# Score products over 128 rows, and pairs of 64-row products issued side by side, in a two-block transformer kernel

## The chip, the core and the metric

The kernel runs on one core of one Trainium2 chip. The metric is device time in microseconds (us) for one execution. A core has a matrix engine (TensorE, in the profile PE, its weight loads PEld), a vector engine (DVE), a scalar engine (ACT), a general engine (POOL), and a queue that issues most transfers (SP). Each engine takes its instructions in the order in which the program has them.

A matrix product reads a stationary operand ("weights", loaded first) and a moving operand. Both lie on up to 128 partitions ("rows"), over which the product sums; the moving operand streams its columns. In the profile `64*128 64x512` is a product over 64 rows with 128 weight columns and 512 moving columns.

## The reference, cut to what matters

Two layers of a first block and one layer of a second, on 512 tokens of width 1024, in float32. Each layer is FFN, mixer, FFN. The mixer of the first block has four groups of four heads of width 64; these three have products over 64 rows:

```
nsa:    s = (q @ k.T) + bias, causal; softmax; o = p @ v        (two branches, and a small compressed one)
gdn:    per chunk of 128 tokens:  K = k @ k.T ,  Q = q @ k.T ,  masked and scaled
mlstm:  S = q @ k.T ;  w = exp(-(M - a)) ;  o = (S * w) @ v ,  causal blocks of 128 tokens
```

The mixer of the second block has 16 heads: 8 "dilated" heads with scores of 128 x 512 per block of 128 queries, and 8 "neighbourhood" heads with scores of 128 x 256.

## The kernel before

Matrix products in float32 run in two ways. Most split each operand into a high part and a rest (`hi`, `lo`, type float32r) and multiply hi*hi, lo*hi and hi*lo, one pass each (`mm3`, lines 308, 311 and 312). Some stay plain float32; the chip runs each of those as two passes, so the profile shows two matrix instructions for one of the program.

**Scores of nsa (lines 1532 and 1533) and of the second block (lines 1708 and 1709).** One head has 64 rows. The first product of a score uses all 128: the query tile holds the high part of a head in one half of its rows and the rest in the other, and the key tile holds the key's high part twice, so one product gives hi*hi + lo*hi. The second product adds q-hi * k-lo and reads only the 64 rows that hold the query's high part. In the second block `parts` (lines 1608 to 1626) makes these tiles: `split` writes `hl`, and four transfers on SP's queue (line 1625) copy halves of it into `two`. The second product reads `hl` itself.

**mlstm (line 1337).** For each head, and each of four key blocks j, one plain float32 product over 64 rows with 512, 384, 256 or 128 columns. Heads 0 and 2 lie on rows 0 to 63, heads 1 and 3 on rows 64 to 127. Heads follow each other.

**gdn (lines 1149 to 1158).** For each chunk and each half u of the rows, four plain float32 products of 64 rows by 128 columns; half 1 comes after half 0.

These parts are Python generators that `par` steps in turn, together with projections that are independent of them. The generators' order gives priorities, and a scheduler fixes each engine's order from priorities, dependences and free buffers. PSUM has two banks for tag `mm` and six for tag `a`, which holds every other product's result.

Of the kernel before, what the change touches and what calls it, by code (L numbers as in the profile page):

```python
# [225 lines left out]
def _body(tc, nc, ctx, I, out):  # L226
# [10 lines left out]
    def nm(s):  # L237
        cnt[0] += 1
        return f"{s}{cnt[0]}"
# [850 lines left out]
    def gdn(blkr, l, MX, m_, n_, q_, s_, c_, t_, out_split, pr, cv, ga, beta, lvl):  # L1090
# [44 lines left out]
        def chunk(c):  # L1135
# [10 lines left out]
            QK[c], BT[c] = m_("qk"), m_("bt")  # L1146
            bs = BT[c]
            g = (V if c < 2 else G).tensor_tensor(q4(bs), q4(seg), b_last(su(beta[:, c]), 128), op=ALU.mult)
            for u in range(2):
                pk = psa()  # L1150
                r = slice(64 * u, 64 * u + 64)
                for b in range(2):
                    PE.matmul(pk[:, b * 128:b * 128 + 128], kT[b][r, ts], kT[b][r, ts], start=True, stop=True)
                    PE.matmul(pk[:, 256 + b * 128:256 + b * 128 + 128], kT[b][r, ts], qT[b][r, ts], start=True,
                              stop=True)
                us = slice(256 * u, 256 * u + 256)
                V.tensor_tensor(bs[:, us], pk[:, 0:256], bs[:, us], op=ALU.mult)
                V.tensor_tensor(QK[c][:, us], pk[:, 256:512], seg[:, us], op=ALU.mult)
                yield
# [127 lines left out]
    def mlstm(sel2, l, MX, m_, n_, q_, s_, c_, t_, out_split, pr, vd, gt, lf):  # L1287

        pi, pf = psa(), psa()
        for i in range(4):  # L1290
            PE.transpose(pi[0:4, i * 128:i * 128 + 128], gt[:, i, 20:24], ident)
            PE.transpose(pf[0:4, i * 128:i * 128 + 128], lf[:, i], ident)
        rw, rM, nF = n_("rw")[0:36], n_("rM")[0:4], n_("nF")[0:4]
        V.memset(rw, 0.0)
        V.tensor_tensor_scan(nF, ones[0:4, 0:1].to_broadcast([4, 512]), pf[0:4, :], 0.0, op0=ALU.mult, op1=ALU.add)
        a = rw[0:4, :]
        V.tensor_tensor(a, pi[0:4, :], nF, op=ALU.add)
        V.tensor_tensor_scan(rM, a, a, 0.0, op0=ALU.max, op1=ALU.max)
        V.tensor_tensor(rw[32:36, :], nF, rM, op=ALU.subtract)
        rr = n_("rr", F32R)[0:36]  # L1300
        S.activation(rr, ones[0:36, 0:1].to_broadcast([36, 512]), AF.Copy, scale=0.0)
        split(rr[0:4], rr[32:36], rM)
        yield
        pc = psa()
        for i in range(4):
            PE.transpose(pc[:, i * 36:i * 36 + 36], rw[:, i * 128:i * 128 + 128], ident[0:36, 0:36])
        ac = t_([128, 4, 36], "ac")
        V.tensor_copy(ac.rearrange("p i r -> p (i r)"), pc[:, 0:144])
        em = t_([128, 4, 4], "em")
        act(em, ac[:, :, 32:36], AF.Exp)  # L1310
        while "d_q1" not in pr:
            yield
        dk, dq = ([pr[f"d_{c}{b}"] for b in range(2)] for c in "kq")
        hn = [n_("hn"), n_("hn")]
        hv = [h_.rearrange("p (i e) -> p i e", i=2) for h_ in hn]
        for h in range(4):
            r, b = slice(64 * (h % 2), 64 * (h % 2) + 64), h // 2
            sel = MX.tile([36, 128], F32R, tag="s", bufs=4, name=nm("sel"))
            V.tensor_copy(sel, b_last(sel2[:, h], 128))
            ps = psa("pM")  # L1320
            PE.matmul(ps, sel, rr, start=True, stop=True)
            pM = n_("pM")
            S.copy(pM, ps)
            yield
            dA, dB, dC = n_("d"), n_("d"), q_("d")
            wt = [dA, dB[:, 0:384], dC, dB[:, 384:512]]
            for j in range(4):
                n = 512 - 128 * j
                aj = ac[:, j, h:h + 1]
                d = wt[j]  # L1330
                V.scalar_tensor_tensor(d[:, 0:128], pM[:, j * 128:j * 128 + 128], aj, mmask, op0=ALU.subtract,
                                       op1=ALU.max)
                act(d[:, 0:128], d[:, 0:128], AF.Exp, scale=-1.0)
                if n > 128:
                    act(d[:, 128:n], pM[:, (j + 1) * 128:512], AF.Exp, scale=-1.0, bias=aj)
                ps = psa("S")
                PE.matmul(ps[:, 0:n], dk[b][r, j * 128:j * 128 + 128], dq[b][r, j * 128:512], start=True, stop=True)  # L1337
                V.scalar_tensor_tensor(d[:, 0:n], ps[:, 0:n], 0.125, d[:, 0:n], op0=ALU.mult, op1=ALU.mult)
                yield
            pn = psa("num")  # L1340
            for i in range(4):
                for j in range(i + 1):
                    PE.matmul(pn[:, i * 65:i * 65 + 65], wt[j][:, (i - j) * 128:(i - j) * 128 + 128], vd[:, j, h],  # L1343
                              start=j == 0, stop=j == i)
            yield
            pv = pn[:, 0:260].rearrange("p (i e) -> p i e", e=65)
            de = c_([128, 4, 2], "de")
            V.tensor_copy(de[:, :, 1], pv[:, :, 64])
            V.scalar_tensor_tensor(de[:, :, 0], de[:, :, 1], -1.0, de[:, :, 1], op0=ALU.mult, op1=ALU.max)
            V.tensor_tensor(de[:, :, 0], de[:, :, 0], em[:, :, h], op=ALU.max)  # L1350
            V.reciprocal(de[:, :, 0], de[:, :, 0])
            t = q_("hq").rearrange("p (i e) -> p i e", i=4)
            V.tensor_tensor(t, pv[:, :, 0:64], b_last(de[:, :, 0], 64), op=ALU.mult)
            q = q_("hq").rearrange("p (i e) -> p i e", i=4)
            S.activation(q, t, AF.Square)
            V.tensor_reduce(de[:, :, 0], q, axis=AX.X, op=ALU.add)
            rsq(de[:, :, 0], de[:, :, 0], 1.0 / 64)
            for g in range(2):
                V.tensor_tensor(hv[g][:, :, h * 64:h * 64 + 64], t[:, 2 * g:2 * g + 2],
                                b_last(de[:, 2 * g:2 * g + 2, 0], 64), op=ALU.mult)  # L1360
            yield
        for b in range(2):
            pt = psa()
            for i in range(4):
                PE.transpose(pt[:, i * 128:i * 128 + 128], hv[i // 2][:, i % 2, b * 128:b * 128 + 128], ident)
            S.activation(dq[b], pt, AF.Identity, scale=C(("mng", l)))
            yield
        while "gates" not in pr:
            yield
        for b in range(2):  # L1370
            out_split(6 + b, dq[b], pr[f"d_o{b}"])
# [48 lines left out]
    def nsa(blkr, l, MX, m_, n_, q_, s_, c_, t_, out_split, pr, hs, cw2, va, sg):  # L1420
# [70 lines left out]
        for h in range(4):  # L1491
# [34 lines left out]
            for br in range(2):  # L1526
                po = psa("o")
                for i in range(4):
                    n = 128 * (i + 1)
                    q = qa[b][:, h % 2, i * 128:i * 128 + 128]  # L1530
                    ps = psa("s")
                    PE.matmul(ps[:, 0:n], q, kk[br][0][:, 0:n], start=True, stop=False)
                    PE.matmul(ps[:, 0:n], q[r], kk[br][1][r, 0:n], start=False, stop=True)  # L1533
                    t = soft_e(n_, c_, ps, n, md[:, 512 - n:512])
                    late.add(unit_b(t, n, po, i, br))
                    if i == 3:
                        late.add(fin(po, h, br), True)
                    yield
# [40 lines left out]
    def _mix2(MX, q0, wf):  # L1579
# [33 lines left out]
        def parts(nat, key, q):  # L1613
            t = m_("qk")
            o, i, r = t, q, box["r"] if key else r8
            if nat and not key:
                o = t.rearrange("p (b r c) -> p r b c", b=4, r=8)
                i, r = (v.rearrange("p (r b c) -> p r b c", r=8, b=4) for v in (q, r))
            V.tensor_tensor(o, i, r, op=ALU.mult)
            hl_ = MX.tile([128, 2, 512], F32R, tag="hl", bufs=4, name=nm("hl"))  # L1620
            two = MX.tile([128, 2, 512], F32R, tag="two", bufs=4, name=nm("two"))
            split(hl_[:, 0], hl_[:, 1], t)
            for u in range(2):
                for v in range(2):
                    nc.sync.dma_start(two.bitcast(F32)[64 * v:64 * v + 64, u], hl_.bitcast(F32)[64 * u:64 * u + 64, 0 if key else u ^ v])
            return two, hl_

        def projv(half, v1, qs, ready=None):
            for c in range(4):
# [71 lines left out]
        late, nat = Late(3, 2), [0]  # L1701

        def scores(n, u, ts, keys, w, bias, nb=1):
            (qa, qh), (ka, kl) = pairs[n]
            r = slice(64 * u, 64 * u + 64)
            ps = psa("s")
            o = ps[:, 0:w] if nb == 1 else ps[:, 0:w].rearrange("p (a b) -> p a b", a=nb)
            PE.matmul(o, qa[:, u, ts], keys(ka[:, u]), start=True, stop=False)
            PE.matmul(o, qh[r, 0, ts], keys(kl[r, 1]), start=False, stop=True)  # L1709
            return soft_e(m_, s_, ps, w, bias)  # L1710

        def dilated():
# [180 lines left out]
```

## Time and profile before

| | us |
|---|---|
| median of 3 runs (lowest to highest) | 3311.61 (3310.05 to 3312.95) |
| the profiled execution: device time | 3313.13 |
| its span in the trace | 3311.4 |
| PE busy in the span | 3242.6 (98%) |
| DVE, ACT, POOL busy | 1723.8, 1212.6, 740.8 |

The granted clock is 0.991 of full speed over the span. A busy time counts overlapping instructions once. A matrix instruction's time contains its way through the array, during which the next one already starts; what it costs is therefore the step from its start to the start of the next, not its duration. The mixers of the first block fill about 508 to 715 us and 1617 to 1824 us of the span, the attention of the second block 2677 to 2880 us.

### The profile page before, as it was taken

How to read it: one execution, taken by the hardware profiler on the slowest of the kernel's cores; microseconds unless marked ns; L12 is line 12 of the kernel's file. 1: busy time of each engine (PE TensorE's matmuls, PEld its weight loads, DVE VectorE, ACT ScalarE, POOL GpSimd, SP SyncE). 2: the span in 40 equal slices, each digit the busy share in tenths (PEclk: the TensorE clock that was granted, in tenths of full speed). 3: DMA queues.
4: the chain of work that ended last, by engine and by line, in shares of the span. 5: the costliest groups of instructions: out<-in, count | busy, mean ns of one | idle time of the engine just before them, and what ended most of it. 6: DMA issues, size and time to landing. Idle time of an engine off the chain costs nothing.

```text
span 3311.4 us, 42958 instructions
## 1 busy us (share of the span) xinstructions
PE 3242.6 (98%) x16168; PEld 2690.1 (81%) x16168; DVE 1723.8 (52%) x2942; ACT 1212.6 (37%) x2287; POOL 740.8 (22%) x754
## 2 busy tenths in 40 slices
PE   7999999999999999999999999999999999999998
PEld 6888887778888888888877888888888877788887
DVE  6555576656555555536655633344543444564433
ACT  3222255453222232224444532233223444652232
POOL 3222222214222222213121322211211300131111
PEclk8999999999999999999999999999999999999999
DMA  6555542114555445534310334333323444342233
GB/s 235 183 167 173 175 143 72 33 45 139 167 168 165 154 143 176 164 117 132 111 34 30 109 100 134 120 118 105 128 97 98 135 148 118 99 139 97 96 94 104
DMA packets 133263, 410.77 MB, mean 124 GB/s; under 512 B 16264, under 2 KB 29708, under 8 KB 132784
## 3 DMA queue, kind: packets, MB, share of 16 engines
q1 hardware_dynamic: 126848, 387.07, 36.1%
q0 software_dynamic: 6064, 20.76, 2.0%
q8 instruction: 127, 2.08, 0.3%
q14 instruction: 80, 0.66, 0.1%
q10 hardware_dynamic: 144, 0.21, 0.0%
HBM read 379.58 MB, written 22.51 MB: 121 GB/s over the span
## 4 chain that ended last, share of the span: by engine, by line
PE 91%; DVE 5%; ACT 2%; issue 1%; POOL 1%; DMA 1%; SPq 0%; DVEq 0%; ACTq 0%; POOLq 0%
PE m L308 14%; PE m L311 14%; PE m L312 14%; PE a L308 11%; PE a L312 11%; PE a L311 11%; PE o L1397 2%; PE pt L1391 2%; DVE lo L297 1%; PE s L1709 1%; PE S L1337 1%; PE a L1191 1%; PE a L1175 1%; PE s L1533 1%; PE num L1343 1%
## 5 line engine op out<-in xcount | busy, mean ns | idle before, releaser
L297 DVE TENSOR_TENSOR lo<-raw,hi 128x512 fp32r<-128x512 f32 (+2 forms) x1056 | 804.9, 767 | 955.2 <-ACT hi L296 930.9
L296 ACT CAST hi<-raw 128x512 fp32r<-128x512 f32 (+2 forms) x1056 | 639.4, 611 | 1653.6 <-PE m L311 902.9
L308 PE MATMUL m<-hh,hi 128*128 128x512 f32 (+1 forms) x1728 | 668.7, 387 | 11.0 <-ACT hh L474 5.3
L311 PE MATMUL m<-hl,hi 128*128 128x512 f32 (+1 forms) x1728 | 661.8, 383 | 5.6 <-DVE hl L633 4.3
L312 PE MATMUL m<-hh,lo 128*128 128x512 f32 (+1 forms) x1728 | 659.8, 382 | 1.8 <-DVE lo L297 1.7
L311 PE MATMUL a<-hl,hi 128*128 128x512 f32 (+1 forms) x1264 | 476.5, 377 | 1.0 <-DVE hl L623 1.0
L308 PE MATMUL a<-hh,hi 128*128 128x512 f32 (+1 forms) x1264 | 476.6, 377 | 0.0
L312 PE MATMUL a<-hh,lo 128*128 128x512 f32 (+1 forms) x1264 | 475.2, 376 | 0.0
L308 PEld LDWEIGHTS m<-hh,hi 128*128 128x128 f32 x1728 | 327.5, 190 | 74.1 <-ACT hh L474 5.5
L311 PEld LDWEIGHTS m<-hl,hi 128*128 128x128 f32 x1728 | 327.4, 189 | 66.5 <-DVE hl L633 5.4
L312 PEld LDWEIGHTS m<-hh,lo 128*128 128x128 f32 x1728 | 327.3, 189 | 64.6 <-DVE lo L297 5.2
L717 POOL TENSOR_SCALAR uh<-u 128x512 fp32r<-128x512 f32 x132 | 112.6, 853 | 1099.9 <-DVE u L710 698.6
L311 PEld LDWEIGHTS a<-hl,hi 128*128 128x128 f32 x1264 | 240.1, 190 | 44.7 <-DVE hl L623 1.8
L312 PEld LDWEIGHTS a<-hh,lo 128*128 128x128 f32 x1264 | 239.9, 190 | 43.2 <-DVE lo L297 0.7
L308 PEld LDWEIGHTS a<-hh,hi 128*128 128x128 f32 x1264 | 240.1, 190 | 42.7 <-ACT hi L296 0.5
L308 PE MATMUL a<-uh,hi 128*128 128x512 f32 (+1 forms) x660 | 229.7, 348 | 0.6
L311 PE MATMUL a<-ul,hi 128*128 128x512 f32 (+1 forms) x660 | 229.5, 348 | 0.0
L312 PE MATMUL a<-uh,lo 128*128 128x512 f32 (+1 forms) x660 | 228.7, 347 | 0.0
L308 PE MATMUL m<-uh,hi 128*128 128x512 f32 x528 | 205.7, 390 | 0.0
L720 POOL TENSOR_TENSOR ul<-u,uh 128x512 fp32r<-128x512 f32 x132 | 203.1, 1538 | 10.8
L312 PE MATMUL m<-uh,lo 128*128 128x512 f32 x528 | 205.4, 389 | 0.0
L311 PE MATMUL m<-ul,hi 128*128 128x512 f32 x528 | 205.4, 389 | 0.0
(462 smaller groups left out, 4012.3 us busy)
## 6 DMA issues: line engine op xcount, KB each, us to landing
raw<-in_ada_dram SPq DMA_DIRECT2D x144, 512.0 KB, 4.3
raw<-in_f1a_dram SPq DMA_DIRECT2D x88, 512.0 KB, 4.2
raw<-in_f2a_dram SPq DMA_DIRECT2D x88, 512.0 KB, 3.7
raw<-in_win_dram SPq DMA_DIRECT2D x48, 512.0 KB, 3.3
raw<-in_g1a_dram SPq DMA_DIRECT2D x44, 512.0 KB, 3.7
raw<-in_g2a_dram SPq DMA_DIRECT2D x44, 512.0 KB, 3.6
raw<-in_f1b_dram SPq DMA_DIRECT2D x32, 512.0 KB, 3.6
raw<-in_f2b_dram SPq DMA_DIRECT2D x32, 512.0 KB, 3.5
```

The source lines that it names most:

```text
L296: order["hi"] = S.copy(h, raw[:, s])
L297: order["lo"] = V.tensor_tensor(l, raw[:, s], h.bitcast(F32), op=ALU.subtract)
L308: i = PE.matmul(o, wh, xh, start=start, stop=False)
L311: PE.matmul(o, wh, xl, start=False, stop=False)
L312: j = PE.matmul(o, wl, xh, start=False, stop=stop)
L717: G.tensor_scalar(uh[:, j], u, 1.0, 0.0, op0=ALU.mult, op1=ALU.add)
L720: order["ul"] = G.tensor_tensor(ul[:, j], u, uh[:, j].bitcast(F32), op=ALU.subtract)
L1175: PE.matmul(p[:, bs_], B[:, bs_], Z[:, bs_], start=True, stop=True)
L1191: PE.matmul(p[:, bs_], RT[:, bs_], w[:, bs_], start=True, stop=True)
L1337: PE.matmul(ps[:, 0:n], dk[b][r, j * 128:j * 128 + 128], dq[b][r, j * 128:512], start=True, stop=True)
L1391: PE.transpose(pt[:, j * 128:j * 128 + 128], t[:, j * 128:j * 128 + 128], ident)
L1397: PE.matmul(o, r[:, j * 128:j * 128 + 128], v, start=j == 0, stop=j == len(vs) - 1)
```

## The change

Second score products read all 128 rows: in nsa the key tile with the rest already held it in both halves; in the second block `parts` makes for each key one more tile, `low`, with four more transfers, and lays out every query as high part over rest. The added term lo*lo comes with it. Tiles `hl` have 2 buffers where they had 4, and `low` has 2. In gdn and mlstm, the products of two heads on the two halves of the rows are issued alternately, each half into a PSUM bank of its own; mlstm works on two heads at a time, with the exponentials of both in a step ahead of the two products, and on the weighted sums of one head after the other.

```diff
@@ gdn, chunk
+            pks = [psa(), psa()]
+            for b in range(2):
+                for o, x in ((0, kT), (256, qT)):
+                    for u in range(2):
+                        r = slice(64 * u, 64 * u + 64)
+                        PE.matmul(pks[u][:, o + b * 128:o + b * 128 + 128], kT[b][r, ts], x[b][r, ts], start=True, stop=True)
             for u in range(2):
-                pk = psa()
-                r = slice(64 * u, 64 * u + 64)
-                for b in range(2):
-                    PE.matmul(pk[:, b * 128:b * 128 + 128], kT[b][r, ts], kT[b][r, ts], start=True, stop=True)
-                    PE.matmul(pk[:, 256 + b * 128:256 + b * 128 + 128], kT[b][r, ts], qT[b][r, ts], start=True,
-                              stop=True)
+                pk = pks[u]
...
@@ mlstm (for each pair b of heads, for each j)
+                pss = [psa("S"), psa("S")]
+                for u in range(2):
+                    r = slice(64 * u, 64 * u + 64)
+                    PE.matmul(pss[u][:, 0:n], dk[b][r, j * 128:j * 128 + 128], dq[b][r, j * 128:512], start=True, stop=True)
+                for u in range(2):
+                    d = wts[u][j]
+                    V.scalar_tensor_tensor(d[:, 0:n], pss[u][:, 0:n], 0.125, d[:, 0:n], op0=ALU.mult, op1=ALU.mult)
+                yield
...
@@ nsa
-                    PE.matmul(ps[:, 0:n], q[r], kk[br][1][r, 0:n], start=False, stop=True)
+                    PE.matmul(ps[:, 0:n], q, kk[br][1][:, 0:n], start=False, stop=True)
...
@@ second block, parts
+            out_ = []
+            for g in range(2 if key else 1):
+                two = MX.tile([128, 2, 512], F32R, tag=("two", "low")[g], bufs=(4, 2)[g], name=nm("two"))
+                for u in range(2):
+                    for v in range(2):
+                        nc.sync.dma_start(two.bitcast(F32)[64 * v:64 * v + 64, u],
+                                          hl_.bitcast(F32)[64 * u:64 * u + 64, g if key else v])
+                out_.append(two)
...
@@ second block, scores
-            PE.matmul(o, qh[r, 0, ts], keys(kl[r, 1]), start=False, stop=True)
+            PE.matmul(o, qa[:, u, ts], keys(kl[:, u]), start=False, stop=True)
```

On PE, in the first mixer where mlstm's first products stand (`S`; `m` is a projection, `s` an nsa score), the program before has:

```order
L312 MATMUL m_5045<-hh,lo_5038 128x512
L1337 MATMUL S_5058<-d_q_4778,d_k_4456 128x512
L1532 MATMUL s_5061<-kk_4286,qa_4339 128x384
L1533 MATMUL s_5061<-kk_4287,qa_4339 128x384
L1397 MATMUL o_4783<-va_3728,pt_4952 128x65 x3
```

and the changed one, with line 1337 now 1344:

```order
L312 MATMUL m_5048<-hh,lo_5045 128x512
L1344 MATMUL S_5149<-d_q_4778,d_k_4456 128x512
L1344 MATMUL S_5150<-d_q_4778,d_k_4456 128x512
L1515 MATMUL a_5163<-kc_3970,a_q_4260 128x32 x4
L1201 MATMUL a_5174<-km,R_5020 128x128 x2
```

Two heads' products stand together. All 16 pairs of the two layers do; one instruction here is two passes on the chip.

On PE, in the second block at the first scores of the third pair of heads (`two_22859` and `two_22871` are the keys' high parts, `hl_22858` and `two_22876` their rests, `pt` are transposes, `o` weighted sums), the program before has:

```order
L1708 MATMUL s_22892<-two_22859,two_22814 128x512
L1709 MATMUL s_22892<-hl_22858,hl_22813 128x512
L1391 MATMUL pt_22899<-km,ts_22771 128x128 x4
L1397 MATMUL o_22731<-vdi_22009,pt_22791 128x65 x4
L1708 MATMUL s_22910<-two_22859,two_22814 128x512
L1709 MATMUL s_22910<-hl_22858,hl_22813 128x512
```

and the changed one:

```order
L1722 MATMUL s_22907<-two_22871,two_22826 128x512
L1402 MATMUL pt_22914<-km,ts_22781 128x128 x4
L1408 MATMUL o_22741<-vdi_22009,pt_22801 128x65 x4
L1722 MATMUL s_22925<-two_22871,two_22826 128x512
L1402 MATMUL pt_22932<-km,ts_22792 128x128 x4
L1408 MATMUL o_22741<-vdi_22009,pt_22812 128x65 x4
L1722 MATMUL s_22943<-two_22871,two_22826 128x512
L311 MATMUL m_23090<-hl,hi_23097 128x512
L312 MATMUL m_23090<-hh,lo_23098 128x512
L1723 MATMUL s_22907<-two_22876,two_22826 128x512
```

The second products of a pair's first scores have moved behind other work. It is so for six of the eight pairs; later scores of a pair have both products together.

On SP's queue, four more transfers stand after the four of each key's high parts, ahead of the next weights.

On PE, in gdn's chunks 0 and 1 (results: `a_4094` and `a_4104` are half 0 of chunk 0 and of chunk 1, `a_4117` and `a_4124` half 1), the program before has:

```order
L1154 MATMUL a_4094<-c_q_3474,c_k_3324 128x128
L1153 MATMUL a_4094<-c_k_3393 128x128
L1154 MATMUL a_4104<-c_q_3474,c_k_3324 128x128
L1154 MATMUL a_4094<-c_q_3576,c_k_3393 128x128
L1153 MATMUL a_4104<-c_k_3393 128x128
L1154 MATMUL a_4104<-c_q_3576,c_k_3393 128x128
L1154 MATMUL a_4117<-c_q_3474,c_k_3324 128x128
L1153 MATMUL a_4117<-c_k_3393 128x128
```

and the changed one (`a_4094` and `a_4095` are the halves of chunk 0, `a_4109` and `a_4110` those of chunk 1):

```order
L1154 MATMUL a_4094<-c_q_3474,c_k_3324 128x128
L1154 MATMUL a_4095<-c_q_3474,c_k_3324 128x128
L1154 MATMUL a_4094<-c_k_3393 128x128
L1154 MATMUL a_4095<-c_k_3393 128x128
L1154 MATMUL a_4094<-c_q_3576,c_k_3393 128x128
L1154 MATMUL a_4095<-c_q_3576,c_k_3393 128x128
L1154 MATMUL a_4109<-c_q_3474,c_k_3324 128x128
L1154 MATMUL a_4110<-c_q_3474,c_k_3324 128x128
```

The halves now alternate. Chunks 2 and 3, between which eleven rows of other work stood in the first layer, follow each other directly.

## Rows read from the trace of the kernel before

**Rows 1.** The page: busy time of each engine, and the chain that ended last

```profile
PE 3242.6 (98%) x16168; PEld 2690.1 (81%) x16168; DVE 1723.8 (52%) x2942; ACT 1212.6 (37%) x2287; POOL 740.8 (22%) x754
...
PE 91%; DVE 5%; ACT 2%; issue 1%; POOL 1%; DMA 1%; SPq 0%; DVEq 0%; ACTq 0%; POOLq 0%
```

**Rows 2.** Windows: length, then busy us (count) of PE, PEld, DVE, ACT, POOL; clock, DMA

```profile
508.00:715.00 207.00, 201.65 (x1228) 159.71 (x1228) 122.69 (x369) 98.86 (x246) 41.91 (x81) 1.00 0.16 49
...
2677.00:2880.00 203.00, 202.44 (x1116) 159.64 (x1114) 95.06 (x251) 105.02 (x204) 18.20 (x19) 1.00 0.40 115
2860.00:2880.00 20.00, 19.77 (x129) 15.80 (x128) 12.79 (x42) 15.36 (x38) 4.19 (x3) 1.00 0.25 76
```

**Rows 3.** Timeline of PE, first scores of the second block: start us, duration us

```profile
2676.89 0.39 PE L312 MATMUL m<-hh,lo 128*128 128x512 f32 x1
2677.11 0.40 PE L1708 MATMUL s<-two,two 128*128 128x512 f32 x1
2677.44 0.49 PE L1709 MATMUL s<-hl,hl 64*128 64x512 f32 x1
...
2680.44 0.50 PE L308 MATMUL m<-hh,hi 128*128 128x512 f32 x1
2680.78 0.60 PE L1391 MATMUL pt<-km,ts 128*128 128x128 f32 x4
```

**Rows 4.** Timeline of PE: 256 columns in an FFN, and a neighbourhood score

```profile
400.45 0.28 PE L308 MATMUL a<-uh,hi 128*128 128x256 f32 x1
400.57 0.28 PE L311 MATMUL a<-ul,hi 128*128 128x256 f32 x1
...
2824.64 0.28 PE L1708 MATMUL s<-two,two 128*128 128x256 f32 x1
2824.85 0.38 PE L1709 MATMUL s<-hl,hl 64*128 64x256 f32 x1
2825.16 0.44 PE L1391 MATMUL pt<-km,ts 128*128 128x128 f32 x2
2825.43 0.56 PE L1397 MATMUL o<-vna,pt 128*128 128x65 f32 x4
```

**Rows 5.** Lines 1533 and 1709: count, duration ns min/median/max, first and last start

```profile
L1533 PE MATMUL s<-kk,qa x64: 323/410/498, 550.6 to 1795.6; 64*128 64x128 f32 x16, 64*128 64x256 f32 x16, 64*128 64x384 f32 x16, 64*128 64x512 f32 x16
...
L1709 PE MATMUL s<-hl,hl x64: 381/438/502, 2677.4 to 2877.7; 64*128 64x512 f32 x32, 64*128 64x256 f32 x32
```

**Rows 6.** Timeline of PE, mlstm's products of 512 and of 128 columns

```profile
595.42 1.12 PE L1337 MATMUL S<-d_q,d_k 64*128 64x512 f32 x2
596.48 0.45 PE L1532 MATMUL s<-kk,qa 128*128 128x384 f32 x1
...
639.40 0.49 PE L1337 MATMUL S<-d_q,d_k 64*128 64x128 f32 x2
639.82 0.45 PE L1532 MATMUL s<-kk,qa 128*128 128x384 f32 x1
```

**Rows 7.** Timeline of PE, gdn: chunks 0 and 1 together, then chunk 2

```profile
508.35 0.72 PE L1153 MATMUL a<-c_k 64*128 64x128 f32 x8
...
510.21 0.27 PE L1153 MATMUL a<-c_k 64*128 64x128 f32 x1
510.21 0.37 PE L1154 MATMUL a<-c_q,c_k 64*128 64x128 f32 x1
...
511.74 0.51 PE L311 MATMUL m<-hl,hi 128*128 128x512 f32 x1
...
582.65 0.48 PE L1153 MATMUL a<-c_k 64*128 64x128 f32 x2
...
584.63 0.55 PE L1239 MATMUL a<-t,XT 128*128 128x64 f32 x3
```

**Rows 8.** SP's timeline (two groups of four copies), and DMA issues: KB, us to landing

```profile
2738.82 7.72 SPq L1625 DMA_DIRECT2D two<-hl  x8
...
two<-hl SPq DMA_DIRECT2D x64, 128.0 KB, 2.3
```

More of the change, by code (lines that the diff above doesn't have):

```diff
@@ L1315, in mlstm @@
         hv = [h_.rearrange("p (i e) -> p i e", i=2) for h_ in hn]
[L1316 to L1326, printed above, removed]
+        for b in range(2):
+            wts, pMs = [], []
+            for u in range(2):
+                sel = MX.tile([36, 128], F32R, tag="s", bufs=4, name=nm("sel"))
+                V.tensor_copy(sel, b_last(sel2[:, 2 * b + u], 128))
+                ps = psa("pM")
+                PE.matmul(ps, sel, rr, start=True, stop=True)
+                pM = n_("pM")
+                S.copy(pM, ps)
+                pMs.append(pM)
+                dA, dB, dC = n_("d"), n_("d"), q_("d")
+                wts.append([dA, dB[:, 0:384], dC, dB[:, 384:512]])
+                yield
@@ L1327, in mlstm @@
             for j in range(4):
                 n = 512 - 128 * j
[L1329 to L1336, printed above, removed]
@@ L1337, in mlstm @@
-                PE.matmul(ps[:, 0:n], dk[b][r, j * 128:j * 128 + 128], dq[b][r, j * 128:512], start=True, stop=True)
-                V.scalar_tensor_tensor(d[:, 0:n], ps[:, 0:n], 0.125, d[:, 0:n], op0=ALU.mult, op1=ALU.mult)
-                yield
[L1340 to L1361, printed above, removed]
+                for u in range(2):
+                    aj, d, pM = ac[:, j, 2 * b + u:2 * b + u + 1], wts[u][j], pMs[u]
+                    V.scalar_tensor_tensor(d[:, 0:128], pM[:, j * 128:j * 128 + 128], aj, mmask, op0=ALU.subtract,
+                                           op1=ALU.max)
+                    act(d[:, 0:128], d[:, 0:128], AF.Exp, scale=-1.0)
+                    if n > 128:
+                        act(d[:, 128:n], pM[:, (j + 1) * 128:512], AF.Exp, scale=-1.0, bias=aj)
@@ new lines, in mlstm @@
+                yield
+                pss = [psa("S"), psa("S")]
+                for u in range(2):
+                    r = slice(64 * u, 64 * u + 64)
+                    PE.matmul(pss[u][:, 0:n], dk[b][r, j * 128:j * 128 + 128], dq[b][r, j * 128:512], start=True, stop=True)
+                for u in range(2):
+                    d = wts[u][j]
+                    V.scalar_tensor_tensor(d[:, 0:n], pss[u][:, 0:n], 0.125, d[:, 0:n], op0=ALU.mult, op1=ALU.mult)
+                yield
+            for u in range(2):
+                h, wt = 2 * b + u, wts[u]
+                pn = psa("num")
+                for i in range(4):
+                    for j in range(i + 1):
+                        PE.matmul(pn[:, i * 65:i * 65 + 65], wt[j][:, (i - j) * 128:(i - j) * 128 + 128], vd[:, j, h],
+                                  start=j == 0, stop=j == i)
+                yield
+                pv = pn[:, 0:260].rearrange("p (i e) -> p i e", e=65)
+                de = c_([128, 4, 2], "de")
+                V.tensor_copy(de[:, :, 1], pv[:, :, 64])
+                V.scalar_tensor_tensor(de[:, :, 0], de[:, :, 1], -1.0, de[:, :, 1], op0=ALU.mult, op1=ALU.max)
+                V.tensor_tensor(de[:, :, 0], de[:, :, 0], em[:, :, h], op=ALU.max)
+                V.reciprocal(de[:, :, 0], de[:, :, 0])
+                t = q_("hq").rearrange("p (i e) -> p i e", i=4)
+                V.tensor_tensor(t, pv[:, :, 0:64], b_last(de[:, :, 0], 64), op=ALU.mult)
+                q = q_("hq").rearrange("p (i e) -> p i e", i=4)
+                S.activation(q, t, AF.Square)
+                V.tensor_reduce(de[:, :, 0], q, axis=AX.X, op=ALU.add)
+                rsq(de[:, :, 0], de[:, :, 0], 1.0 / 64)
+                for g in range(2):
+                    V.tensor_tensor(hv[g][:, :, h * 64:h * 64 + 64], t[:, 2 * g:2 * g + 2],
+                                    b_last(de[:, 2 * g:2 * g + 2, 0], 64), op=ALU.mult)
+                yield
@@ L1619, in parts @@
             V.tensor_tensor(o, i, r, op=ALU.mult)
-            hl_ = MX.tile([128, 2, 512], F32R, tag="hl", bufs=4, name=nm("hl"))
-            two = MX.tile([128, 2, 512], F32R, tag="two", bufs=4, name=nm("two"))
+            hl_ = MX.tile([128, 2, 512], F32R, tag="hl", bufs=2, name=nm("hl"))
             split(hl_[:, 0], hl_[:, 1], t)
[L1623 to L1626, printed above, removed]
+            out_ = []
+            for g in range(2 if key else 1):
+                two = MX.tile([128, 2, 512], F32R, tag=("two", "low")[g], bufs=(4, 2)[g], name=nm("two"))
+                for u in range(2):
+                    for v in range(2):
+                        nc.sync.dma_start(two.bitcast(F32)[64 * v:64 * v + 64, u],
+                                          hl_.bitcast(F32)[64 * u:64 * u + 64, g if key else v])
+                out_.append(two)
+            return out_
         def projv(half, v1, qs, ready=None):
@@ L1703, in scores @@
         def scores(n, u, ts, keys, w, bias, nb=1):
-            (qa, qh), (ka, kl) = pairs[n]
-            r = slice(64 * u, 64 * u + 64)
+            (qa,), (ka, kl) = pairs[n]
             ps = psa("s")
```

## The prediction

> **What bounds the kernel now.** I read the page first: PE is busy for 98% of the span and makes 91% of the chain that ended last, so a step that PE no longer makes shortens the run unless another engine is late there [rows 1]. Then the windows over the three stretches that the change touches: 207 us in each first-block mixer (the second layer's reads as the first's) and 203 us in the second block's attention. PE is busy for 201.65 of 207 and 202.44 of 203 us there; DVE has 122.69 and 95.06, ACT 98.86 and 105.02 [rows 2]. PE is the bound in both, with room on the others. Last the timeline of PE, from start to start, since a drain of the array hides inside a busy time.
>
> There the reader is to see what a 64-row product costs between 128-row ones. A 512-column product starts 0.22 us after the one before (2676.89 to 2677.11; I use 0.225). With a 64-row product next, the step is 0.33, since that one waits until the array is empty; the 64-row product and the 128-row ones behind it take 0.42 to 0.43, since each also has its weights loaded only after that wait. Nine products of 512 columns, four of them over 64 rows, take 2680.78 - 2677.11 = 3.67 us, against 9 x 0.225 = 2.03: 0.41 us for each change to 64 rows and back [rows 3].
>
> **The score products (lines 1533 and 1709).** There are 64 + 64 of them [rows 5]. The 128-row product that replaces one has as many columns and reads the weights' tile that the first product read; it streams as long and needs no drain. So the whole excess goes: 0.41 us where products of 512 columns stand around it. For 256 columns, between a first product and two transposes, the three groups take 2825.43 - 2824.64 = 0.79 us; without switches they take two steps of 0.12 (400.45 to 400.57) and two of about 0.11 (a float32 pass of 128 columns, below), 0.46. The excess is 0.33 [rows 4]. Most stand ahead of transposes or weighted sums, so I take 0.35: 128 x 0.35 = 44.8 us, bounds 128 x 0.33 = 42 and 128 x 0.41 = 52.
>
> **mlstm (line 1337).** One head takes 596.48 - 595.42 = 1.06 us for 512 columns and 639.82 - 639.40 = 0.42 for 128 [rows 6]; 384 and 256 I put on the line between, so four products take 2 x 1.48 = 2.96 us. If the two heads of a pair run beside each other, one of each pair costs nothing: 4 x 2.96 = 11.8 us over both layers. Sixteen entries and exits go too, about 0.17 each (0.10 of drain ahead, 0.06 to 0.11 of load behind): 2.7. Sum 14.5 us. The lower bound, if they run one after the other, is the 2.7.
>
> That halves run beside each other the old order shows in one place, where chunks 0 and 1 of gdn meet: two passes start at 510.21, a line-1153 one of 0.27 us and a line-1154 one of 0.37, and eight passes of 0.27 or more take 0.72 together [rows 7].
>
> **gdn (lines 1153 and 1154).** Chunk 2 alone takes 584.63 - 582.65 = 1.98 us for 16 passes, about 0.11 each plus the entry; chunk 3 has the same, elsewhere. Their 32 passes now stand together in two streams of 16, 1.95 us in place of 3.96. Chunks 0 and 1 take 511.74 - 508.35 = 3.39 us, of which about 0.3 waits for an input; two streams need 1.95 + 0.3, and 1.1 go. That is 3.1 a layer, 6.2 in all; the lower bound is 0, if nothing more overlaps.
>
> Gross: 44.8 + 14.5 + 6.2 = 65.5 us.
>
> **What comes back.** First, the `low` copies. Eight keys have four more copies of 128 KB; eight copies hold SP for 7.72 us, so about 1 us each at most there, and 2.3 us pass from issue to landing [rows 8]. On SP, the next weights and the next pair's copies stand behind them. A second product can thus come 2 to 4 us later than its first could. The changed order puts about 4 us or more of PE's other products between the two in six of the eight pairs (in the piece shown, transposes and weighted sums of 32 passes at 0.11 and five steps of 0.225: 4.6 us), and the first two pairs' copies stand long ahead of their use. I price this at 2 us; with no cover it is 8 x 4 = 32, without any delay 0.
>
> Second, the other engines. In the last 20 us of the attention, where projections no longer fill PE, ACT has 15.36 us of work [rows 2]. Thirteen of these excursions lie there, 4.5 us: PE's 20 would fall to 15.5, what ACT needs without any wait. I give back 2 us there. Elsewhere DVE and ACT go from about 60% to about 66% of the stretch; a score's softmax comes due a little earlier against the same latency. mlstm now holds two banks for its S, and gdn two for a chunk, of the six. I take a tenth of the gross for both, 6 us, bounds 0 and 15.
>
> Net: 65.5 - 2 - 2 - 6 = 55.5, say 56 us. The profiled execution took 3313.13 us, 1.7 of it outside the span and not touched, and is 1.5 above the median; 3313.1 - 56 = 3257 for it, 3311.6 - 56 = 3255.6 for the median. I predict 3256.
>
> **Where the Trainium skill says otherwise.** The rows show that a pass over one half starts while passes over the other that stand earlier in the order have not started: in the old order every first-half product of chunks 0 and 1 stands ahead of the second half's line-1154 ones, and yet at 510.21 a pass of line 1154 starts with the longer duration of a first one, beside a line-1153 one [rows 7]; I read it as the second half's. The skill's "TensorE: Matmul & The Clock Gate", Part 3 ("The mechanism"), says that matmuls are strictly first in, first out in start and end. By that rule head u = 1 could not start before the second pass of head u = 0, a pair would take three passes' time rather than two, and mlstm would give 5.9 + 2.7 instead of 14.5: the sum would be about 50. The trace disagrees with the rule here, so it has a small chance.
>
> The step of 0.22 us between 128-row products of different weights leaves no room for a load that waits for the array [rows 3]. The same section says that a weight load overlaps running matmuls only when its row group differs. By that rule the second 128-row product would still have its load exposed, about the 0.1 us by which steps after a switch exceed steps before one (0.43 and 0.33), and 128 x 0.1 = 13 of the 44.8 would stay. The trace disagrees: lines 308, 311 and 312 follow each other all over the run without it.
>
> **Rivals.**
> 1. The halves run one after the other at these sizes: mlstm gives 2.7, gdn nothing; 44.8 + 2.7 - 8 = 39.5, so 3272. For it: mlstm's passes are up to four times as long as gdn's, and the trace has no pair of that size. Against: gdn's rows. Chance 0.08.
> 2. In-order starts, as above: 3256 + 6 = 3262. For it: the S pair stands as two passes of one head, then two of the other. Against: the start at 510.21. Chance 0.06.
> 3. Exposed loads, as above: 3256 + 13 = 3269. For it: the steps behind a switch, 0.1 longer. Against: the 0.22 between main products. Chance 0.03.
> 4. Chains take over: the copies' delay and softmax latencies keep PE waiting, at half of the bounds or more (16 + 2 + 15): 65.5 - 33 = 32, so 3279. For it: the order was laid out anew in all three stretches, and ACT's share at the end. Against: PE finds other work everywhere but in the last 20 us. Chance 0.09.
> 5. Slower: SP becomes the bound of the attention. Weights stand behind the copies, and the copies behind their high parts; if a key's delay reaches weights that PE needs next, PE stands for the copies and again for the weights. It decides from 65.5 / 8 = 8.2 us lost per key, against 2 to 4 us of extra queue. With 10 us per key the run is 80 - 65.5 = 14 us longer, 3326. Against: 32 copies of 1 us are 32 of 203 us, and SP's earlier 64 left PE busy throughout. Chance 0.03.
> That the change does not bring the products together is excluded by the order.
>
> **How the numbers follow.** The forecast has 0.71; its own range, from the bounds of the score products and of what comes back, is 3244 (52 in place of 44.8, and half of the losses) to 3268. Rivals 1 to 4 lie at 3262 to 3279 with 0.26 together, rival 5 has 0.03. The range for 8 in 10 is 3242 to 3277: it leaves out rival 5, the outer part of rival 4, and as much at the lower end. What this kernel's measurement can tell from no change is about 0.2%, 7 us: faster 0.95, of all but rival 5 and the far end of rival 4; within 0.2% 0.02; slower 0.03.
>
> **What would show it.** Right: second score products that start 0.22 us (512 columns) or 0.12 us (256) after the first where both stand together; two S passes starting within some 0.02 us of each other, and a pair of 512 columns taking 1.1 us in all; a chunk's 16 passes in about 1 us; PE busy still near 98%. Wrong: S pairs that take 2.1 us (rival 1) or 1.6 (rival 2); a step of 0.33 between two 128-row products (rival 3); PE idle ahead of second products, released by a DMA, or longer waits by DVE or ACT for each other inside the attention (rival 4); PE waiting for `lo` of projection weights behind SP's copies (rival 5).

## The result, and the profile after

The changed kernel takes 3260.14 us (median of 4 runs, 3254.45 to 3261.70) against 3311.62 (4 runs on the same chip): 51.5 us less; the ratio of the means is 0.9842, 95% interval 0.9825 to 0.9859. The forecast was 3256, in a range of 3242 to 3277. The profiled execution took 3260.46 us, with a span of 3258.7 against 3311.4, so 52.7 us can be followed in the two traces.

The page after, busy time of each engine and the chain that ended last [rows 1]:

```profile
PE 3184.6 (98%) x16168; PEld 2676.0 (82%) x16168; DVE 1725.5 (53%) x2942; ACT 1211.0 (37%) x2287; POOL 744.1 (23%) x754
...
PE 90%; DVE 4%; ACT 2%; POOL 2%; issue 1%; DMA 1%; SPq 0%; DVEq 0%; ACTq 0%; POOLq 0%
```

PE has the same 16168 instructions and is busy 58.0 us less; the other engines' work is as before. 58.0 - 52.7 = 5.3 us more are idle time of PE. Followed by the number of its products in the two traces, 2.2 us of it lie near the end of the attention (14067th to 14194th product) and 0.8 in the two mixers. The rest is a balance between stretches that the change does not touch (among them 2.9 more ahead of the 1000th product, 2.2 less between the 12900th and the first score of the second block).

Three windows of the trace after, each from the PE instruction at which a window of [rows 2] began to the one at which it ended (length, then busy us and count of PE, PEld, DVE, ACT, POOL; granted clock, DMA share, GB/s):

```profile
508.65:698.65 190.00, 183.76 (x1228) 155.45 (x1227) 123.21 (x370) 98.38 (x243) 43.31 (x81) 0.99 0.17 54
2641.40:2827.00 185.60, 182.68 (x1115) 159.50 (x1114) 98.45 (x251) 104.18 (x203) 18.74 (x19) 0.99 0.53 146
2806.25:2827.00 20.75, 18.28 (x129) 16.18 (x128) 14.83 (x42) 15.65 (x37) 4.69 (x3) 0.92 0.44 115
```

The mixer is 17.0 us shorter and the second block's attention 17.4. But the last 20 us of the attention are not shorter at all: 20.75 against 20.00, with PE busy for 18.28 of them and a clock of 0.92.

The timeline of PE in the trace after (start, duration), at the places of [rows 3], [rows 4], [rows 6] and [rows 7]:

```profile
580.77 0.49 PE L1154 MATMUL a<-c_k 64*128 64x128 f32 x4
...
582.43 0.39 PE L1154 MATMUL a<-c_q,c_k 64*128 64x128 f32 x4
582.75 0.99 PE L1240 MATMUL a<-t,XT 128*128 128x64 f32 x7
...
598.08 1.13 PE L1344 MATMUL S<-d_q,d_k 64*128 64x512 f32 x4
599.04 0.97 PE L1515 MATMUL a<-kc,a_q 64*128 64x32 f32 x8
...
2641.41 0.40 PE L1722 MATMUL s<-two,two 128*128 128x512 f32 x1
2641.65 0.40 PE L1723 MATMUL s<-two,two 128*128 128x512 f32 x1
2641.88 0.40 PE L1722 MATMUL s<-two,two 128*128 128x512 f32 x1
...
2771.20 0.28 PE L1722 MATMUL s<-two,two 128*128 128x256 f32 x1
2771.31 0.29 PE L1723 MATMUL s<-two,two 128*128 128x256 f32 x1
2771.44 0.39 PE L311 MATMUL m<-hl,hi 128*128 128x512 f32 x1
```

The steps that were to show are there. Two heads' S products of 512 columns, four passes, take 599.04 - 598.08 = 0.96 us; the mixer's other pair of 512 columns, ahead of a 128-row product, takes 1.06, as much as one head's two passes took alone [rows 6]. In the 0.05 us from 598.05 to 598.10 two passes start:

```profile
598.08 0.70 PE L1344 MATMUL S<-d_q,d_k 64*128 64x512 f32 x2
```

So it is with 12 of the 16 pairs. In two pairs of each layer, one of 384 and one of 256 columns, the second head starts 0.27 to 0.30 us after the first. One of 384 columns takes 605.50 - 604.66 = 0.84 us with both starting together, and 660.22 - 659.11 = 1.11 so:

```profile
604.66 0.92 PE L1344 MATMUL S<-d_q,d_k 64*128 64x384 f32 x4
605.50 0.70 PE L1535 MATMUL oc<-vc,pcT 128*128 128x256 f32 x2
...
659.11 1.18 PE L1344 MATMUL S<-d_q,d_k 64*128 64x384 f32 x4
660.22 0.51 PE L311 MATMUL m<-hl,hi 128*128 128x512 f32 x1
```

The 32 passes of chunks 2 and 3 take 582.75 - 580.77 = 1.98 us, what chunk 2 alone took [rows 7]. A second score product of 512 columns follows the first after 0.24 us and is followed after 0.23; of 256 columns, 0.11 and 0.13.

Where the gain lies, by the start times of PE products of the same number in the two traces (the counts are equal), beside the prediction's gross terms (0.35 us for each score product) and what is left when its tenth, its 2 us for the copies and its 2 us for the tail are taken off:

| stretch | before | after | gain | predicted gross, net |
|---|---|---|---|---|
| mixer of layer 0 (2200th to 3700th) | 263.70 | 246.12 | 17.6 | 21.5, 19.4 |
| mixer of layer 1 (7700th to 9300th) | 284.40 | 267.07 | 17.3 | 21.5, 19.4 |
| second block, first score to 14067th | 183.01 | 164.84 | 18.2 | 18.6, 14.7 |
| second block, 14067th to 14300th | 42.30 | 43.47 | -1.2 | 3.9, 1.5 |

Of the second block's 64 excursions (64-row products among 128-row ones) 53 lie in its first row and 11 in its second; the prediction counted 13 at the end. The other 0.8 us of the 52.7 lie elsewhere. Two stretches give less than was forecast: the mixers, and the end of the attention. The experiments are about these two, and about the three parts of the change.

### The profile page after: what moved, and what is told of

Read it like the earlier page. It is cut to its first block, busy times and chain, and to the rows that moved or that the text cites. A ratio compares the mean times of both kernels' runs of the same rounds, so it can differ in the third digit from the quotient of the medians.

```text
span 3258.7 us, 43061 instructions
## 1 busy us (share of the span) xinstructions
PE 3184.6 (98%) x16168; PEld 2676.0 (82%) x16168; DVE 1725.5 (53%) x2942; ACT 1211.0 (37%) x2287; POOL 744.1 (23%) x754
## 4 chain that ended last, share of the span: by engine, by line
PE 90%; DVE 4%; ACT 2%; POOL 2%; issue 1%; DMA 1%; SPq 0%; DVEq 0%; ACTq 0%; POOLq 0%
PE m L311 14%; PE m L312 14%; PE m L308 14%; PE a L308 11%; PE a L312 11%; PE a L311 11%; PE o L1408 2%; PE pt L1402 1%; DVE lo L297 1%; PE a L1176 1%; PE a L1192 1%; PE num L1354 1%; DVE t L621 0%; DVE hl L623 0%; PE hid L947 0%
```

## The experiments

Each was run four times or more beside the kernel before on the same chip; a gain is the difference of the medians, a ratio that of the means. The table's stretches, read in each run's one trace, show where it lies.

**One: the score products alone (scores_only).** The kernel before with this, and the copies that go with it:

```diff
-                    PE.matmul(ps[:, 0:n], q[r], kk[br][1][r, 0:n], start=False, stop=True)
+                    PE.matmul(ps[:, 0:n], q, kk[br][1][:, 0:n], start=False, stop=True)
...
-            PE.matmul(o, qh[r, 0, ts], keys(kl[r, 1]), start=False, stop=True)
+            PE.matmul(o, qa[:, u, ts], keys(kl[:, u]), start=False, stop=True)
```

> The 128-row score products alone, with gdn and mlstm as before. If the parts add up (theory: each change to 64 rows and back costs 0.35 to 0.40 us, and PE is the bound), the 128 products remove 45 to 50 us from PE, and 5 to 7 come back at the end of the second block's attention: 3265 to 3275, a gain of 37 to 43. If the gain of the whole change came mostly from the pairs (rival), this would gain under 25: over 3287.

Measured: 3274.63 us against 3315.55, 40.9 less; ratio 0.9877 [0.9862, 0.9891].

**Two: the pairs of gdn and mlstm alone (pairs_only).** The rest of the change, with the score products as before.

> The paired products of gdn and mlstm alone, with the scores' second products over 64 rows as before. Theory: mlstm gives 14 to 15 us, gdn's chunks 2 and 3 give 4, gdn's chunks 0 and 1 give nothing and cost up to 3 through a longer idle time of PE there: 3294 to 3299, a gain of 13 to 18. Rival, in which the pairs' gain is eaten by waits for two heads' exponentials at a time: a gain under 8, over 3304.

Measured: 3300.92 against 3315.55, 14.6 less; ratio 0.9957 [0.9942, 0.9972]. Both gains lie where the theories put them, and 40.9 + 14.6 = 55.5 is close to the 51.5 and 50.8 of the two measurements of the whole change: the parts add up, near enough.

**Three and four: mlstm alone, gdn alone (mlstm_only, gdn_only).** Each has the part of the diff in that function, and nothing else.

> The kernel before with the change's mlstm alone: the two heads of a pair stand next to each other; gdn and all score products as before. It splits the 14.6 us that the pairs of mlstm and gdn gave together. The prediction's terms (mlstm 14.5, gdn 6.2 us) less what its switches' neighbours give back: 13 to 15 us faster. Theory from the trace after (chunks 0 and 1 of gdn gain nothing, since transposes wait for DVE just as long, and chunks 2 and 3 give 2 us a layer): mlstm alone 10 to 13 us, and with the other run the sum is the 14.6. Rival (the coupling of the heads makes DVE and ACT late, which uses up part of mlstm's own gain): under 9 us.

> The kernel before with the change's gdn alone: the 16 products of a chunk in halves that alternate; mlstm and all score products as before. Prediction: 6.2 us faster. Theory from the trace after: 2 to 5 us (two layers of 2 us by chunks 2 and 3, and nothing, or a loss at the lower clock, by chunks 0 and 1). Rival (nothing overlaps between chunks, or what does is waited for again): within 1.5 us of the kernel before.

Measured (5 runs of mlstm, 11 of gdn, 15 of the kernel before) against 3315.33: mlstm 3301.96, 13.4 less, within the prediction's 13 to 15, ratio 0.9963 [0.9949, 0.9976]; gdn 3314.27, 1.1 less, ratio 0.9999 [0.9991, 1.0008], which is no change: the 2 to 5 us of the theory did not come, and the rival's "within 1.5 us" did. So nearly all that the pairs give is mlstm's. Per mixer, by the start times of the table's first row, scores alone give 10.6 us, mlstm alone 6.5 and gdn alone 0.5: 17.6, the gain of the whole change. There is no loss between the parts to look for; gdn itself gives too little. The timeline of PE in gdn alone, where chunks 0 and 1 end, shows why:

```profile
511.08 0.39 PE L1154 MATMUL a<-c_q,c_k 64*128 64x128 f32 x4
511.40 0.50 PE L311 MATMUL m<-hl,hi 128*128 128x512 f32 x1
...
512.44 0.39 PE L312 MATMUL m<-hh,lo 128*128 128x512 f32 x1
512.67 0.40 PE L308 MATMUL m<-hh,hi 128*128 128x512 f32 x1
515.65 0.66 PE L1163 MATMUL a<-km,bt 128*128 128x128 f32 x2 [2.58 <-DVE bt L1158]
...
516.53 0.63 PE L312 MATMUL m<-hh,lo 128*128 128x512 f32 x1
516.96 0.63 PE L308 MATMUL m<-hh,hi 128*128 128x512 f32 x1
```

PE is through with its products, runs six passes of projections, and then waits 2.58 us for DVE. After that wait, equal passes start 0.43 us apart instead of 0.23.

**Five: chunks 0 and 1 as before (gdn_late).** The changed kernel, but these two chunks do one half after the other; chunks 2 and 3 keep the alternating order.

```diff
+            pks = {}
             for u in range(2):
+                if c < 2 or not u:
+                    for v in (u,) if c < 2 else range(2):
+                        pks[v] = psa()
```

> The changed kernel with gdn's chunks 0 and 1 as before (one half after the other), chunks 2 and 3 in alternation. Theory: in the changed kernel PE idles 2.58 us ahead of the transposes of chunk 0 (1.70 before) and then runs at half clock for 3.4 us in each layer; here the idle time is 1.7 us again, the clock stays at 1.00, and 1.5 us a layer come back: 3255 to 3259. Rival: the half clock came by chance, from where the stretch fell; then no change, 3260, and an idle time near 1.7 us with half clock, or without it in the changed kernel's other runs.

Measured: 3255.91 (3254.43 to 3258.41) against 3315.55, ratio 0.9821 [0.9806, 0.9836]. The mixers gain 19.1 us each instead of 17.6 and 17.3, so putting these two chunks side by side cost 1.5 to 1.8 us in each. As a gain over the changed kernel that is small beside the spread of the runs: the two ratios' intervals overlap. The windows of 2 us from 512 on (length, PE busy and count, granted clock, DMA), of before, of the changed kernel and of this one:

```profile
512.00:514.00 2.00, 1.42 (x6) 1.00 0.00 0
514.00:516.00 2.00, 0.88 (x5) 1.00 0.00 0
516.00:518.00 2.00, 2.00 (x13) 1.00 0.00 0
```

```profile
512.00:514.00 2.00, 1.19 (x6) 1.00 0.00 0
514.00:516.00 2.00, 0.23 (x1) 0.90 0.00 0
516.00:518.00 2.00, 2.00 (x7) 0.50 0.00 0
518.00:520.00 2.00, 2.00 (x10) 0.75 0.00 0
```

```profile
514.00:516.00 2.00, 1.20 (x7) 1.00 0.00 0
516.00:518.00 2.00, 2.00 (x13) 1.00 0.00 0
```

In the changed kernel PE is granted 0.50, the 1.2 GHz level, right after its long wait, and does 7 products in 2 us where it otherwise does 13. With the old order of two chunks the clock stays at 1.00. This is no chance of one trace. In all six traces with the two chunks side by side and nothing put into the wait (the changed kernel's, gdn_only, pairs_only, after_again, low_free, tail_direct), in both layers, PE waits 2.58 or 2.59 us and around its end the clock falls to 0.50 for some 3.4 us. In all five with the old order (before, scores_only, mlstm_only, gdn_late, both_fixes) it waits 1.70 to 1.73 us, and 1.00 stays.

That the products' end does not set the transposes' start is seen in the timelines. PE's, before and after:

```profile
513.02 0.40 PE L308 MATMUL m<-hh,hi 128*128 128x512 f32 x1
515.12 0.41 PE L1162 MATMUL a<-km,bt 128*128 128x128 f32 x2 [1.70 <-DVE bt L1157]
```

```profile
508.97 0.71 PE L1154 MATMUL a<-c_k 64*128 64x128 f32 x8
...
511.54 0.50 PE L311 MATMUL m<-hl,hi 128*128 128x512 f32 x1
...
512.80 0.39 PE L308 MATMUL m<-hh,hi 128*128 128x512 f32 x1
515.77 0.66 PE L1163 MATMUL a<-km,bt 128*128 128x128 f32 x2 [2.58 <-DVE bt L1158]
```

And DVE's, before:

```profile
510.92 1.75 DVE L1148 TENSOR_TENSOR bt<-lg,sg 128x512 f32<-128x512 f32 x1 [1.16 <-POOL lg L1144]
512.60 0.78 DVE L297 TENSOR_TENSOR lo<-raw,hi 128x512 fp32r<-128x512 f32 x1
513.30 0.41 DVE L1157 TENSOR_TENSOR bt<-a,bt 128x256 f32<-128x256 f32 x1
```

After:

```profile
511.56 1.77 DVE L1148 TENSOR_TENSOR bt<-lg,sg 128x512 f32<-128x512 f32 x1 [1.17 <-POOL lg L1144]
513.25 0.78 DVE L297 TENSOR_TENSOR lo<-raw,hi 128x512 fp32r<-128x512 f32 x1
513.95 0.41 DVE L1158 TENSOR_TENSOR bt<-a,bt 128x256 f32<-128x256 f32 x1
```

Both traces have the same chain, 0.64 us apart, which is about how far the whole stage is apart (first gdn product at 508.35 and at 508.97). DVE waits for POOL's `lg`, not for PE, before it can touch a chunk. The products take 511.54 - 508.97 = 2.57 us instead of 3.39, and products that are done 0.8 us sooner are read no sooner.

**Six: more work into the wait (gdn_yield).** The changed kernel, with chunks 0 and 1 giving way three times between products and transposes:

```diff
+            if c < 2:
+                yield
+                yield
+                yield
             pt = psa()
```

> The changed kernel with three more steps of the other generators between the products of gdn's chunks 0 and 1 and the transposes that wait for DVE: nine more projection products stand ahead of the transposes. Theory: the idle time of 2.58 us falls to about 0.5, the clock stays at 1.00: 2 x (2.0 + 1.5) = 7 us less, if what is used up here is not missed later in the mixer: 3253 to 3257. Rival: the mixer is bound by gdn's own chain of steps, and projection work moved ahead leaves PE idle at the mixer's end: no change, 3259 to 3261.

Measured: 3260.41 against 3315.55, ratio 0.9833 [0.9817, 0.9849]: not better than the changed kernel. The waits in its gdn are down to 0.50 and 0.91 us, and the clock stays at 1.00 there. But some of the projections that now fill them are missing 165 us later, where the same mixer's output waits for DVE (its timeline of PE):

```profile
679.26 0.39 PE L311 MATMUL m<-hl,hi 128*128 128x512 f32 x1
681.10 0.33 PE L1565 MATMUL a<-km,ov 128*128 128x128 f32 x1 [1.45 <-DVE ov L1561]
```

In the changed kernel that wait is 0.97. Nearer to the rival: work moved forward leaves holes where it stood, and PE's idle time in the first mixer is 7.95 us against 7.70 in all. That is not the whole account. The mixer takes 246.3 us against 246.1, so what the full clock should have given back, some 1.5 us, is gone as well; the new order has one change to 64 rows more (some 0.4 us), and where the rest went was not followed.

**Seven: the changed kernel again, beside the next three (after_again).**

> The changed kernel itself once more, as a yardstick on the chip of the following runs. All theories: ratio to before 0.982 to 0.986.

Measured: 3263.20 (3260.14 to 3264.16) against 3313.96, ratio 0.9843 [0.9826, 0.9859], as the first time.

**Eight: without the low copies (low_free).**

```diff
-            for g in range(2 if key else 1):
+            for g in range(1):
...
-            PE.matmul(o, qa[:, u, ts], keys(kl[:, u]), start=False, stop=True)
+            PE.matmul(o, qa[:, u, ts], keys(ka[:, u]), start=False, stop=True)
```

> The changed kernel without the low copies: in the second block the second score product reads the key's high part once more, so the term with the key's rest is left out of the scores. It shows what the 32 copies cost. Theory (the order keeps other work between the two products): 0 to 2 us less than the changed kernel, no wait of PE for a transfer. Rival (the copies are where the second block loses): 4 us or more less.

Measured: 3259.87 against 3313.96, ratio 0.9835 [0.9821, 0.9850]; 3.3 us below the changed kernel measured beside it, between the two expectations, with intervals that overlap. In its trace the 127 products at the end of the attention (14067th to 14194th) take 17.5 us, against 20.0 before, 20.8 and 19.1 in the two traces of the changed kernel. That is 1.6 to 3.3 us less, and only there: the 987 products of the attention ahead of them take 164.65 us without the copies and 164.84 and 164.50 with them. It is not shown that the copies cost this much. In the changed kernel's first trace PE waits for no copy at the tail, and a stretch at 0.50 lies in its 20.8 us; without the copies the clock stays at 1.00 there, and the wait for `hl` is 1.2 us.

**Nine: a shorter chain at the tail (tail_direct).** For the dilated output ACT writes the high part straight from PSUM and DVE takes the rest from PSUM as well, without a tile between:

```diff
-                    S.activation(t, pt, AF.Identity, scale=C("dig", b))
+                    S.activation(h, pt, AF.Identity, scale=k)
+                    V.scalar_tensor_tensor(hl[:, 4 + b], pt, k, h.bitcast(F32), op0=ALU.mult, op1=ALU.subtract)
```

> The changed kernel, in which the dilated group's normalised output goes from PSUM to its high part by ACT in one step, and its rest is taken by DVE from PSUM (one ACT step of 0.62 us less for each of four tiles, and a chain shorter by as much). Theory: at the end of the attention PE waits 1.8 us for this chain, since it now gets there sooner than ACT and DVE; the wait falls to below 1 us, the clock stays at 1.00 there: 1 to 3.5 us less than the changed kernel. Rival: PE waits there for the softmax of the last scores, whatever this chain does; no change.

Measured: 3262.42 against 3313.96, ratio 0.9840 [0.9826, 0.9855]: no gain, as the rival had it. The wait for `hl` is still 1.8 us in its trace.

**Ten: both (both_fixes).** Experiments five and nine together.

> gdn's chunks 0 and 1 as before the change, chunks 2 and 3 alternating, and the shorter chain at the end of the attention. Theory: the two places are apart from each other, so their gains add: 4 to 7 us less than the changed kernel, ratio to before 0.980 to 0.983. Rival: one of the two is made up for elsewhere; no better than gdn_late alone (0.982).

Measured: 3256.81 (3252.42 to 3258.93) against 3313.96, ratio 0.9823 [0.9808, 0.9838]: 6.4 us below the changed kernel measured beside it. That is within the theory's 4 to 7, but it is also experiment five's ratio of 0.9821 alone, as the rival had it, and the trace has nothing from the tail: the 127 products take 21.8 us. Its waits of PE against those of others, all from 2640 to 2900 us, the second block's attention and what follows it (PE's product and line, what it waited for: us in total, times, longest). The changed kernel, which has none of 0.2 us or more for a copy:

```profile
PE m L311 <- DVE hl L800: 2.1, 2, 1.8
```

The changed kernel's second trace:

```profile
PE s L1723 <- DMA two<-hl: 1.0, 1, 1.0
PE m L311 <- DVE hl L800: 0.9, 1, 0.9
```

The shorter chain alone:

```profile
PE m L311 <- DVE hl L1799: 1.8, 1, 1.8
```

Both fixes:

```profile
PE s L1726 <- DMA two<-hl: 1.8, 1, 1.8
...
PE m L311 <- DVE hl L1802: 0.2, 1, 0.2
```

The wait for `hl` is all but gone, and a wait for a low copy of the same length stands in its place: PE comes to a second score product sooner than its copy lands. At the end of the attention two things are late at about the same time, the copies and the chain of ACT and DVE. That the shorter chain made the one wait into the other is not shown: the same chain alone left the wait for `hl` as it was, and the changed kernel's own second trace has some of both. In the traces of the changed kernel and its variants these 127 products take 17.5 to 21.8 us.

## Why the prediction was right, and where it was wrong

**What bounds the kernel.** PE did, and does: 98% of the span, 90% of the chain. 52.7 us of the 65.5 that were to go came off the span.

**The score products.** Right, and to the size: the 53 of the second block that precede its tail give 183.01 - 164.84 = 18.2 us, 0.34 each, against 0.35. In the mixers 64 of them give 10.60 + 10.54 us, 0.33 each. Alone they are worth 40.9 us of the 44.8; the tail took most of the rest (20.0 us before, 18.9 in scores_only, for 11 of them).

**mlstm.** Right: halves run beside each other at 512 columns too, and 13.4 us of 14.5 came (13.0 by the mixers' traces). Rivals 1 and 2 needed a pair to take 2.1 or 1.6 us; it took 0.96 to 1.06. Of the 0.7 us a layer that are missing, two late starts of some 0.26 make 0.5. At 659.38 the second head's weight load waits for a semaphore that ACT raises at 659.34, at the end of an instruction that reads another product out of PSUM; this looks like a bank that comes free late, which the prediction priced only as part of its tenth. The rule on which rival 2 stood, strict order in start and end (the Trainium skill, "TensorE: Matmul & The Clock Gate", Part 3), would have the second head's first pass wait for the first head's second; the trace disagrees. So the sentence on the chip, that each engine takes its instructions in the program's order, does not hold for the starts of PE's passes on opposite halves, as [rows 7] already showed. Rival 3, with the same section's rule that loads overlap only between row groups, wanted a step of 0.33 between two 128-row products; the trace disagrees with 0.24 and 0.11. That section names a second case, a load into a background weight buffer, which the prediction left out; with it the steps agree.

**gdn.** The step that failed. The 2.0 us a layer of chunks 2 and 3 came: 32 passes take 1.98 us, and of gdn_late's 19.1 us a mixer the scores' 10.6 and mlstm's 6.5 leave 2.0. "Two streams need 1.95 + 0.3, and 1.1 go" did not. PE's products there did end earlier, by 0.8 us (2.57 for 3.39; eight of the 32 passes ran in two streams already before). But the path there runs through POOL and DVE, which the prediction did not follow; the transposes start 6.77 us after the stage's first product before (515.12 - 508.35) and 6.80 after (515.77 - 508.97). PE's wait grew from 1.70 to 2.58, and the half clock behind it took at least 1.5 us more: 2.0 - 1.5 = 0.5 a layer, which gdn alone shows. The trace of before had the wait of 1.70 us just behind the rows that the prediction read; its releaser would have said that the 1.1 us can't be had.

**What comes back.** About the right sum for partly wrong reasons. I spread a tenth, 6 us, over softmax chains and banks everywhere; what is missing in a mixer against 21.5 gross is 2.6 at gdn, 0.7 at mlstm and 0.6 at the scores. The tail was priced at 2 us, which would have left 17.5 of PE's 20. Its thirteen excursions were eleven, 3.9 us and not 4.5, and it took 20.8 in the profiled execution, so all of that and 0.8 more came back there, in waits for `hl` (and in other traces for copies) and at the half clock. The copies were priced at 2 us as delays spread over six pairs; the stretch ahead of the tail lost nothing to them in the changed kernel, and what they cost at the tail is open. That the sum came within 4 us of the forecast is in part luck: of the 65.5 some 13 came back where 10 were taken off, and most of it for other reasons.

**Rivals 4 and 5.** Rival 4 is what happened on a small scale, in two places, by 2.2 us of idle time at the tail and 0.8 in the mixers beside the clock, not 33. Rival 5 did not occur: no wait of PE for `lo` of the projections' weights of 0.2 us or more in the attention.

**Open.** How the tail's loss divides between copies, chain and half clock: it changes from run to run, and no run took the copies and the longer chain away together. gdn_late is the best kernel measured, but by little: 0.9821 against 0.9842 is some 7 us, and both_fixes is 6.4 us below the changed kernel measured beside it, where the intervals reach about 5 us to each side; the mixers' 1.5 to 1.8 us a layer are what the traces show of it.

## What to carry to other kernels

Among 128-row products, one over 64 rows costs more than a 128-row one with operands filled up, here 0.33 to 0.34 us each; and two 64-row products on opposite halves next to each other cost what one did, where both can start at once. But ask at each such place who reads the product and when that reader is free: where it waits for a third engine, a faster product only makes PE wait longer. Where several things are late at one place, measure with all of them removed before mending one, which was not done here.

## What the runs showed of the hardware that was not expected

A longer wait of PE cost more than its length. After the 2.58 us at gdn the granted clock was 0.50 (1.2 GHz) and steps took 0.43 us instead of 0.23, until about 519; after 1.70 us at the same place, in the kernel before and in gdn_late, it stayed at 1.00. A clock of 0.50 behind a wait was seen in the second block too, as in the kernel with both fixes after its wait of 1.76 us for the low copy (windows of its PE):

```profile
2812.00:2816.00 4.00, 3.28 (x14) 0.67 0.27 98
2816.00:2820.00 4.00, 4.00 (x20) 0.50 0.00 0
```

The changed kernel's second profile has a wait of 1.03 us for a low copy, at 2817, and kept 1.00; so did gdn_yield's after 1.64 us for one, at 2797. An equal wait of 1.95 us in an FFN, at 420 to 422 us (line 586), was followed by 0.50 in the trace before and by 1.00 in the changed kernel's first. Which waits are followed by a lower clock these runs do not settle; that a change which shortens the work in front of a wait can pay 1.5 us for the longer wait, they do.
